# A second way to split weight pieces: casting and adding DMAs for every other piece of the mixer phases

## The chip, the cores and the metric

One NeuronCore of a Trainium2 chip runs the whole program. The metric is the device time of one execution in microseconds (us). Engines are named as in the profile: PE (TensorE, matmuls), PEld (its weight loads, which overlap PE), DVE (VectorE), ACT (ScalarE), POOL (GpSimd) and SP (SyncE). A difference of about 0.2% is what a measurement of this kernel can tell.

## The reference

Two layers of a decoder trunk on 272 tokens (16 meta tokens and 256 of input) and a width of 1024, in float32. Cut to what matters:

```
for l in range(DEPTH):                       # 2 layers
    u = rms_norm(x, norm1_g[l]) @ w_in[l]    # 1024 x 6560
    (u_conv, c_q, c_kv, k_rope, hq, hf, hi, hg, u_gate) = split(u)
    y_a = conv_module(u_conv, ...)           # gated causal depthwise conv, layer norm, swish, projection
    y_b = mla(c_q, c_kv, k_rope, ...)        # latent attention, 8 heads, projection
    y_c = hgrn2(hq, hf, hi, hg, ...)         # gated linear recurrence, 4 heads, projection
    mix = gates[0] * y_a + gates[1] * y_b + gates[2] * y_c
    x = x + mix @ w_out[l]
    x = x + square(relu(rms_norm(x, norm2_g[l]) @ w_ff1[l])) @ w_ff2[l]
```

## The kernel before

Activations lie transposed in SBUF (features on partitions, tokens along the row). All the large products run on PE with both operands split into a high and a low part of type float32r; `mm3` (L218) adds three matmuls, high x high, low x high and high x low. The weights come as **pieces** of 128 x 1024 float32 (512 KB): one piece feeds 8 steps of 128 rows, 24 matmuls of up to 272 columns. There are 276 of them.

`piece` (L204) fetches a piece by a DMA on SP's queue into `wraw` (3 buffers, `fetch`, L104), rounds it on ACT into `whi` (L209, 4 buffers) and takes the difference on DVE into `wlo` (L211, 4 buffers). A slot of `whi` and `wlo` comes free when the last matmul that reads the piece has run. `piece` raises the priority of these steps by 500, so the planner of the language puts them as early as buffers allow. The planner lays out the order of every engine's queue ahead of time by its own simulated times; each engine then works its queue strictly in order.

Each layer has a mixer phase and a feed-forward phase. In the mixer phase a hand-written list `dense` (L1008) sets the order of weight products: tiles of `w_in` by `win_acc` (L367), first 7 latent pieces (j below NLAT = 8), then the head tiles to j = 27, then 24 gate tiles; with the last gate tiles the `merge_tile` products (L982) alternate, each piece of the branch projections (`wbr`) serving two of them. Between these, four streams of smaller steps (latent, HGRN, attention, convolution) are woven in at set rates (L1015 to L1028). They use DVE and ACT heavily, and POOL for a few things: powers of -0.5 for norms (`rsqrt`, L238, and L912), clearing `kl` (L799) and copying `qm` (L851). Pieces of `wuq` and `wukv` go through the same four slots. The evacuations of PSUM go over ACT (L412 to L435, L980) and DVE (L996); `win_acc` uses two PSUM banks `acc`, in the latent part `hx` too. The feed-forward phase (L1038 to L1095), `wout`, `wff1` and `wff2`, uses 72 pieces in each layer.

Of the kernel before, what the change touches and what calls it, by code (L numbers as in the profile page):

```python
# [10 lines left out]
F32 = mybir.dt.float32  # L11
# [3 lines left out]
AF = mybir.ActivationFunctionType  # L15
# [24 lines left out]
NLAT = 8  # L40
# [46 lines left out]
def block_kernel(ctx, tc, xT_d, pp_d, cc_d, win_d, wuq_d, wukv_d, wbr_d, wout_d, wff1_d, wff2_d, out_d):  # L87
    nc = tc.nc
    pe, act, dve, pool = nc.tensor, nc.scalar, nc.vector, nc.gpsimd
    MUL, ADD, SUB = ALU.mult, ALU.add, ALU.subtract  # L90
# [13 lines left out]
    def fetch(src, n=1024):  # L104
        raw = wsp.tile([P, 1024], F32, name="wraw", tag="wraw")
        nc.sync.dma_start(out=raw[:, :n], in_=src[:, :n])
        return raw
# [3 lines left out]
    with tc.high_priority(offset=2 * AHEAD):  # L111
        nc.scalar.dma_start(out=pp, in_=pp_d)
        for j in range(4):
            nc.sync.dma_start(out=xT[:, 2 * j:2 * j + 2, :], in_=xT_d[:, 2 * j:2 * j + 2, :])
            if j == 0:
                first = {"kr": fetch(win_d[0, 0], KD * ROPE), "kv": fetch(win_d[0, 1])}
# [72 lines left out]
    def psum_acc():  # L189
        return ps_acc.tile([P, 512], F32, name="acc", tag="acc")  # L190
# [4 lines left out]
    def psum_hx():  # L195
        return ps_hx.tile([P, 512], F32, name="hx", tag="hx")
# [4 lines left out]
    def psum_sm():  # L201
        return ps_sm.tile([P, 512], F32, name="sm", tag="sm")

    def piece(src, raw=None):  # L204

        with tc.high_priority(offset=AHEAD):
            raw = raw or fetch(src)
            hi = wsp.tile([P, 1024], F32R, name="whi", tag="whi", bufs=4)
            act.copy(out=hi, in_=raw)  # L209
            lo = wsp.tile([P, 1024], F32R, name="wlo", tag="wlo", bufs=4)  # L210
            dve.tensor_tensor(out=lo, in0=raw, in1=hi.bitcast(F32), op=SUB)  # L211
        return hi, lo

    def split(hi, lo, src):
# [3 lines left out]
    def mm3(out, whi, wlo, xhi, xlo, start, stop):  # L218
        pe.matmul(out, whi, xhi, start=start, stop=False)  # L219
        pe.matmul(out, wlo, xhi, start=False, stop=False)  # L220
        pe.matmul(out, whi, xlo, start=False, stop=stop)  # L221
# [62 lines left out]
    def scale_input(xg, l, k):  # L284
# [16 lines left out]
                      in1=lb[:, 5, :].unsqueeze(1).broadcast_to([P, 2, HH]), op=MUL)  # L301
# [5 lines left out]
    for l in range(DEPTH):  # L307
# [33 lines left out]
        def unit(name, dt=F32):  # L341
            return t4.tile([P, HH, L], dt, name=name, tag="u")
# [22 lines left out]

        tiles = win_tiles()
        def win_acc(j, n0):  # L367
            hi, lo = piece(win_d[l, j], first["kv"] if l == 0 and j == 1 else None)
            xh, xl = xg if j < NLAT else (hhi, hlo)
            ps = psum_hx() if j < NLAT and j % 2 == 0 else psum_acc()  # L370
            for k in range(KD):
                o = k * P
                mm3(ps[:, :L - n0], hi[:, o:o + P], lo[:, o:o + P], xh[:, k, n0:], xl[:, k, n0:],
                    k == 0, k == KD - 1)
            return ps
# [22 lines left out]
        def head_tile(j):  # L398
            kind, i, _, _ = tiles[j]
            if kind == "kr":  # L400
                rope_keys(j)
                return
            n0 = T0 if kind in ("q", "g") else 0
            ps = win_acc(j, n0)[:, :L - n0]
            with tc.high_priority(offset=200):
                take(kind, i, ps, n0)
# [40 lines left out]
        def latent_steps():  # L447
# [44 lines left out]
            for g in range(2):  # L492
                uqhi, uqlo = piece(wuq_d[l, g])
                for h in range(4):
                    ps = psum_mx()[:, :L]
                    for j in range(2):
                        o = j * 512 + h * P
                        mm3(ps, uqhi[:, o:o + P], uqlo[:, o:o + P], cqhi[:, j, :], cqlo[:, j, :], j == 0, j == 1)
                    act.activation(out=msq_[:QK, h, :], in_=ps[:QK], func=AF.Square)
                    dve.tensor_tensor(out=qT[g][:, h, :], in0=ps, in1=csg, op=MUL)  # L500
                    yield
                with together():
                    for h in (3, 2, 1, 0):
                        pe.matmul(sums[32 * h:32 * h + 32, :L], sel96[:QK, g, :], msq_[:QK, h, :], start=(g == 0), stop=(g == 1))
                yield
# [3 lines left out]
            for w in qtiles:  # L509
# [10 lines left out]
                                     in1=heads(ra[:, 1, q0:3]), op0=MUL, op1=MUL)  # L520

            ukhi, uklo = piece(wukv_d[l])
            kT = [unit(f"kT{g}") for g in range(2)]
            vv = [half(f"vv{w}", "vv", 3) for w in range(3)]
# [449 lines left out]
        mix = {}  # L974

        def gate_tile(i):

            ps = win_acc(N_HEAD_TILES + i, T0)
            gates[i] = gp.tile([P, L], F32, name="gate", tag="gate")
            act.activation(out=gates[i][:, :N], in_=ps[:, :N], func=AF.Tanh, scale=0.5)  # L980

        def merge_tile(i):  # L982
            b, m = divmod(i, KD)
            yh, yl = ys[BRANCHES[b]]
            if i == 0:
                mix["sum"] = [unit(f"mix{j}") for j in range(2)]
            if i % 2 == 0:
                mix["w"] = piece(wbr_d[l, i // 2])
            bhi, blo = mix["w"]
            ps = (psum_acc, psum_hx, psum_hx)[b]()  # L990
            for k in range(4):
                o = (i % 2 * 4 + k) * P
                mm3(ps[:, :N], bhi[:, o:o + P], blo[:, o:o + P], yh[:, k, T0:], yl[:, k, T0:], k == 0, k == 3)
            g, total = gates[i], mix["sum"][m // 4][:, m % 4, :N]
            with tc.high_priority(offset=AHEAD):
                dve.scalar_tensor_tensor(out=total if b == 0 else g[:, :N], in0=g[:, :N], scalar=1.0, in1=ps[:, :N], op0=ADD, op1=MUL)  # L996
            if b > 0:
                dve.tensor_tensor(out=total, in0=total, in1=g[:, :N], op=ADD)  # L998
            if b == 2:
                if m == 0:  # L1000
                    mix["hi"] = actp.tile([P, KD, L], F32R, name="mhi", tag="ahi")
                    mix["lo"] = actp.tile([P, KD, L], F32R, name="mlo", tag="alo")
                act.activation(out=mix["hi"][:, m, T0:], in_=total, func=AF.Copy, scale=0.5)
                dve.scalar_tensor_tensor(out=mix["lo"][:, m, T0:], in0=total, scalar=0.5, in1=mix["hi"][:, m, T0:].bitcast(F32),
                                         op0=MUL, op1=SUB)
# [3 lines left out]
        for i in range(3 * KD):  # L1009
            dense.append((merge_tile, i))  # L1010
            if i + NGATE < 3 * KD:
                dense.append((gate_tile, i + NGATE))
# [193 lines left out]
```

## Time and profile before

| | us |
|---|---|
| median of 3 runs | 961.36 (961.18 to 961.63) |
| the profiled execution | 961.29 |
| its span, first to last instruction | 959.5 |
| PE busy | 931.0 |
| DVE busy | 716.5 |
| ACT busy | 526.3 |
| POOL busy | 50.7 |

Busy time counts an engine's instructions, not its waits. In a group of lines, "idle before" is the time for which the engine stood just before these instructions, with what ended it; in a timeline the same stands in square brackets. PE's matmuls are pipelined, so a matmul's own duration (about 290 ns) overlaps the next; some 0.12 us lie between two starts. Granted clock 1.00 is TensorE's full clock.

The kernel's phases can be told by the stretch: up to about 280 us the first layer's mixer phase, to about 482 its feed-forward phase, to about 760 the second mixer phase, then the second feed-forward phase.

### The profile page before, as it was taken

The numbers are of one execution on the slowest core, as the hardware profiler recorded it, in microseconds if no ns is written. First come the engines' busy times: TensorE is split into PE (matmuls) and PEld (weight loads), VectorE is DVE, ScalarE is ACT, GpSimd is POOL, SyncE is SP. The second block draws the span as 40 slices with busy tenths as digits, with TensorE's granted clock in tenths as the row PEclk, the third lists the DMA queues.
The fourth block names the chain that finished last, engine by engine and source line by source line (L and its number), as shares of the span: only waits on it lengthen the run. The fifth ranks groups of instructions, "written<-read, shape, count | busy, mean of one in ns | idle before, by whom it ended". The sixth has DMA issues, their size and how long they took to land. (4 is left out here: it accounts for less than half of the span.)

```text
span 959.5 us, 18623 instructions
## 1 busy us (share of the span) xinstructions
PE 931.0 (97%) x7474; PEld 896.2 (93%) x7474; DVE 716.5 (75%) x1348; ACT 526.3 (55%) x945; POOL 50.7 (5%) x87
## 2 busy tenths in 40 slices
PE   6999999899999999999999999997998999999998
PEld 6899999779999999999999889896897999999998
DVE  7799999976887766555557998999668887665552
ACT  6467665554546555544445587665444566663331
POOL 3004000000000000000010021000000000000000
PEclk9999999989999999999999999998999999999999
DMA  8454433414445555555454444333144466555661
GB/s 264 131 176 140 147 133 111 133 34 142 163 148 178 194 176 177 176 176 176 160 172 158 141 145 155 130 132 113 67 146 163 155 195 199 179 190 187 198 203 56
DMA packets 42422, 149.16 MB, mean 155 GB/s; under 512 B 4704, under 2 KB 6368, under 8 KB 42336
## 3 DMA queue, kind: packets, MB, share of 16 engines
q1 hardware_dynamic: 40608, 146.10, 46.2%
q10 hardware_dynamic: 1728, 1.88, 0.6%
q8 instruction: 58, 0.95, 0.4%
q14 instruction: 28, 0.23, 0.1%
HBM read 146.91 MB, written 1.05 MB: 154 GB/s over the span
## 5 line engine op out<-in xcount | busy, mean ns | idle before, releaser
L209 ACT CAST whi<-wraw 128x1024 fp32r<-128x1024 f32 x276 | 289.3, 1049 | 340.4 <-PE acc L221 191.2
L211 DVE TENSOR_TENSOR wlo<-wraw,whi 128x1024 fp32r<-128x1024 f32 x276 | 337.6, 1223 | 167.0 <-ACT whi L209 165.4
L219 PE MATMUL acc<-hhi,whi 128*128 128x272 f32 (+1 forms) x704 | 205.1, 292 | 2.3 <-ACT scrahi L417 1.6
L221 PE MATMUL acc<-hlo,whi 128*128 128x272 f32 (+1 forms) x704 | 202.7, 289 | 0.2 <-DVE hlo L216 0.2
L220 PE MATMUL acc<-hhi,wlo 128*128 128x272 f32 (+1 forms) x704 | 202.2, 287 | 0.0
L219 PEld LDWEIGHTS acc<-hhi,whi 128*128 128x128 f32 x704 | 132.6, 188 | 6.6 <-ACT scrahi L417 1.8
L221 PEld LDWEIGHTS acc<-hlo,whi 128*128 128x128 f32 x704 | 132.4, 188 | 2.5 <-issue 0.9
L220 PEld LDWEIGHTS acc<-hhi,wlo 128*128 128x128 f32 x704 | 132.6, 188 | 1.2 <-issue 0.4
L935 DVE SCALAR_TENSOR_TENSOR cacc<-hpad,pph,cacc 128x272 f32<-128x272 f32 (+1 forms) x240 | 111.0, 485 | 0.7
L220 PE MATMUL acc<-xhi,wlo 128*128 128x272 f32 (+1 forms) x256 | 73.4, 287 | 0.0
L220 PE MATMUL hx<-xhi,wlo 128*128 128x272 f32 (+1 forms) x256 | 73.2, 286 | 0.0
L221 PE MATMUL acc<-xlo,whi 128*128 128x272 f32 (+1 forms) x256 | 73.1, 286 | 0.0
L221 PE MATMUL hx<-xlo,whi 128*128 128x272 f32 (+1 forms) x256 | 72.9, 285 | 0.0
L220 PE MATMUL hx<-fhi,wlo 128*128 128x272 f32 (+1 forms) x256 | 72.9, 285 | 0.0
L220 PE MATMUL acc<-fhi,wlo 128*128 128x272 f32 (+1 forms) x256 | 72.9, 285 | 0.0
L219 PE MATMUL acc<-fhi,whi 128*128 128x272 f32 (+1 forms) x256 | 72.8, 284 | 0.0
L219 PE MATMUL hx<-fhi,whi 128*128 128x272 f32 (+1 forms) x256 | 72.8, 284 | 0.0
L221 PE MATMUL acc<-flo,whi 128*128 128x272 f32 (+1 forms) x256 | 72.7, 284 | 0.0
L221 PE MATMUL hx<-flo,whi 128*128 128x272 f32 (+1 forms) x256 | 72.7, 284 | 0.0
L219 PE MATMUL acc<-xhi,whi 128*128 128x272 f32 (+1 forms) x256 | 72.7, 284 | 0.0
L219 PE MATMUL hx<-xhi,whi 128*128 128x272 f32 (+1 forms) x256 | 72.7, 284 | 0.0
L221 PEld LDWEIGHTS acc<-xlo,whi 128*128 128x128 f32 x256 | 48.3, 189 | 0.1
(375 smaller groups left out, 2097.3 us busy)
## 6 DMA issues: line engine op xcount, KB each, us to landing
wraw<-in_wff_dram SPq DMA_DIRECT2D x128, 512.0 KB, 3.4
wraw<-in_win_dram SPq DMA_DIRECT2D x102, 512.0 KB, 3.4
wraw<-in_wbr_dram SPq DMA_DIRECT2D x24, 512.0 KB, 3.3
wraw<-in_wout_dram SPq DMA_DIRECT2D x16, 512.0 KB, 3.3
wraw<-in_wuq_dram SPq DMA_DIRECT2D x4, 512.0 KB, 3.2
xT<-in_xT_dram SPq DMA_DIRECT2D x4, 272.0 KB, 5.4
wraw<-in_wukv_dram SPq DMA_DIRECT2D x2, 512.0 KB, 3.7
out_dram<-xT ACTq DMA_DIRECT2D x8, 128.0 KB, 2.4
```

The lines of the kernel that those rows point to most:

```text
L209: act.copy(out=hi, in_=raw)
L211: dve.tensor_tensor(out=lo, in0=raw, in1=hi.bitcast(F32), op=SUB)
L219: pe.matmul(out, whi, xhi, start=start, stop=False)
L220: pe.matmul(out, wlo, xhi, start=False, stop=False)
L221: pe.matmul(out, whi, xlo, start=False, stop=stop)
L935: dve.scalar_tensor_tensor(out=a, in0=hpad[:, c, T0 + k:T0 + k + N], scalar=hpar(l, "cw", c * CK + k), in1=a, op0=MUL, op1=ADD)
```

## The change

`piece` gets a flag. With it, the piece isn't fetched into `wraw`: a DMA on POOL's queue reads the float32 weights from HBM and writes them as float32r into `whi` (a cast), ACT writes the negative of `whi` into `wlo`, and a second DMA on POOL's queue reads the same weights again and adds them to `wlo`. The flag is set for odd j from 9 on in `win_acc` (22 pieces in a layer) and for every second `wbr` piece (6 in a layer), 56 of 276 pieces. All others are made as before.

```diff
-    def piece(src, raw=None):
+    def piece(src, raw=None, adding=False):
         with tc.high_priority(offset=AHEAD):
-            raw = raw or fetch(src)
             hi = wsp.tile([P, 1024], F32R, name="whi", tag="whi", bufs=4)
-            act.copy(out=hi, in_=raw)
             lo = wsp.tile([P, 1024], F32R, name="wlo", tag="wlo", bufs=4)
-            dve.tensor_tensor(out=lo, in0=raw, in1=hi.bitcast(F32), op=SUB)
+            if adding:
+                nc.gpsimd.dma_start(out=hi, in_=src)
+                act.activation(out=lo, in_=hi.bitcast(F32), func=AF.Copy, scale=-1.0)
+                nc.gpsimd.dma_start(out=lo, in_=src, accum_op=ADD)
+            else:
+                raw = raw or fetch(src)
+                act.copy(out=hi, in_=raw)
+                dve.tensor_tensor(out=lo, in0=raw, in1=hi.bitcast(F32), op=SUB)
         return hi, lo
...
-            hi, lo = piece(win_d[l, j], first["kv"] if l == 0 and j == 1 else None)
+            hi, lo = piece(win_d[l, j], first["kv"] if l == 0 and j == 1 else None, j >= NLAT and j % 2 == 1)
...
-                mix["w"] = piece(wbr_d[l, i // 2])
+                mix["w"] = piece(wbr_d[l, i // 2], adding=i % 4 == 2)
```

## Rows read from the trace of the kernel before

**Rows 1.** The page: span, and busy us (share), instructions, by engine.
```profile
span 959.5 us, 18623 instructions
...
PE 931.0 (97%) x7474; PEld 896.2 (93%) x7474; DVE 716.5 (75%) x1348; ACT 526.3 (55%) x945; POOL 50.7 (5%) x87
```

**Rows 2.** Busy time by stretch, from the span's start; clock, DMA share, GB/s.
```profile
84.00:172.00 88.00, 88.00 (x720) 83.45 (x720) 82.70 (x199) 55.36 (x128) 6.33 (x8) 1.00 0.40 133
172.00:206.00 34.00, 28.51 (x212) 23.91 (x211) 29.88 (x79) 19.07 (x49) 1.29 (x2) 0.90 0.24 77
...
276.00:480.00 204.00, 204.00 (x1623) 203.92 (x1622) 130.22 (x187) 105.41 (x162) 0.00 (x0) 1.00 0.53 174
...
507.00:562.00 55.00, 53.44 (x414) 49.64 (x413) 47.65 (x102) 36.19 (x59) 6.14 (x3) 1.00 0.42 137
...
658.00:684.00 26.00, 20.44 (x152) 16.34 (x152) 20.90 (x55) 13.33 (x34) 0.63 (x1) 0.80 0.17 60
684.00:752.00 68.00, 64.18 (x524) 61.39 (x523) 50.10 (x90) 30.49 (x48) 2.71 (x3) 1.00 0.45 149
```

**Rows 3.** PE's timeline around the longest hole of each layer: start, duration.
```profile
191.29 1.12 PE L844 MATMUL hx<-q,k 128*64 128x64 f32 x8 [3.28 <-DVE k L840]
...
666.89 1.12 PE L844 MATMUL hx<-q,k 128*64 128x64 f32 x8 [2.81 <-DVE k L840]
```

**Rows 4.** Busy time in short stretches at these holes; the clock stands third from last.
```profile
186.00:190.00 4.00, 0.96 (x5) 0.57 (x5) 4.00 (x13) 2.60 (x8) 0.29 (x1) 1.00 0.16 36
190.00:198.00 8.00, 6.24 (x36) 4.46 (x36) 8.00 (x25) 4.16 (x14) 0.00 (x0) 0.57 0.14 50
664.00:676.00 12.00, 7.61 (x44) 5.55 (x43) 10.91 (x32) 4.58 (x14) 0.63 (x1) 0.57 0.12 44
```

**Rows 5.** Costliest groups (the two of `piece`), and the cast's waits (us, times, longest).
```profile
L211 DVE TENSOR_TENSOR wlo<-wraw,whi 128x1024 fp32r<-128x1024 f32 x276 | 337.6, 1223 | 167.0 <-ACT whi L209 165.4
L209 ACT CAST whi<-wraw 128x1024 fp32r<-128x1024 f32 x276 | 289.3, 1049 | 340.4 <-PE acc L221 191.2 <-PE hx L221 97.0 <-issue 37.5
...
ACT whi L209 <- PE acc L221: 191.2, 129, 4.2
...
ACT whi L209 <- DMA wraw<-in_win_dram: 3.7, 4, 1.2
```

**Rows 6.** L106: all fetches; those of 84 to 172 us; landing times, all, then that stretch.
```profile
L106 SPq DMA_DIRECT2D wraw<-in_win_dram x104: 327/328/487, 1.2 to 707.5; - x104
...
DMA to landing us min/median/max: 2.8/3.4/6.6
...
DMA to landing us min/median/max: 3.1/3.3/3.9
```

**Rows 7.** POOL's timeline from 60 to 260 us: start, duration, idle before.
```profile
72.62 2.90 POOL L238 TENSOR_TENSOR ks<-ks,mhalf 128x8 f32<-128x8 f32 x1 [26.33 <-DVE ks L557]
...
85.00 1.64 POOL L238 TENSOR_TENSOR ks<-ks,mhalf 128x8 f32<-128x8 f32 x1 [1.85 <-DVE rq L519]
...
186.39 0.29 POOL L851 COPY qm<-q 128x128 f32<-128x128 f32 x1 [16.84 <-DVE q L839]
```

**Rows 8.** Timelines of ACT and PE: two pieces' casts and their first matmuls.
```profile
222.22 1.05 ACT L209 CAST whi<-wraw 128x1024 fp32r<-128x1024 f32 x1 [2.37 <-PE acc L221]
...
228.61 0.39 PE L219 MATMUL acc<-hhi,whi 128*128 128x272 f32 x1
...
97.66 1.04 ACT L209 CAST whi<-wraw 128x1024 fp32r<-128x1024 f32 x1 [0.58 <-PE acc L221]
...
110.38 0.37 PE L219 MATMUL acc<-hhi,whi 128*128 128x272 f32 x1
```

**Rows 9.** Line 209 alone by stretch: length, ACT busy and casts, clock, DMA share, GB/s.
```profile
84.00:172.00 88.00, 23.07 (x22) 1.00 0.40 133
...
206.00:276.00 70.00, 21.00 (x20) 1.00 0.43 144
...
562.00:658.00 96.00, 27.87 (x27) 1.00 0.42 143
...
684.00:752.00 68.00, 20.01 (x20) 1.00 0.45 149
```

**Rows 10.** The first layer's wukv piece on PE: duration min/median/max, first and last start.
```profile
L541 PE MATMUL hx<-whi,kvm x1: 398/398/398, 62.5 to 62.5; 128*128 128x512 f32 x1
...
L543 PE MATMUL hx<-wlo,mla_hi x2: 392/446/499, 64.6 to 84.3; 128*128 128x512 f32 x2
```

## The prediction

> **What bounds the kernel now.** I read the page's busy table first [rows 1]: PE is busy 931.0 of 959.5 us, DVE 716.5, ACT 526.3, POOL 50.7. The reader is to see that PE is nearly the whole span, so no change off PE gives much unless it closes a hole in PE. The profiled execution took 961.29 us, 1.8 us more than its span; the median of the runs is 961.36, so sums made against the profile carry over as they are.
>
> The busy table by stretch shows where holes are [rows 2]. In 84 to 172 us PE never rests, but DVE works 82.7 of 88 us. In 172 to 206 PE loses 5.5 us, in 658 to 684 5.6, in 684 to 752 3.8 and in 507 to 562 1.6: 16.5 us in all. What ends PE's wait is DVE: the longest is 3.28 us before L844, released by DVE L840, and its twin in the second layer 2.81 us [rows 3]. Around each the granted clock, 1.00 (2.4 GHz) before, falls towards 0.50 (1.2 GHz): its mean is 0.57 over 8 us and over 12 us [rows 4], so 0.43 x 20 = 8.6 us of PE's work is lost to the clock. All that a lighter DVE can give back is thus some 16.5 + 8.6 = 25 us.
>
> Last I looked at the weight ring. The groups of lines give 276 casts (L209, 1049 ns) and 276 subtractions (L211, 1223 ns) [rows 5]. The commonest wait of the cast is on PE's L221, 191.2 us in 129 times: the cast waits for a slot of whi to be given back, not for its DMA, for which the first such row has 3.7 us [rows 5]. So the ring of four is full, and a piece has from the release of its slot until PE reaches it. I call that its room.
>
> **The change, part by part.** 28 pieces per layer change (22 of win, 6 of wbr), 56 of 276.
>
> Removed: 56 x 1.223 = 68.5 us of DVE, all in the mixer phases, and 56 fetches from SP's queue. Replaced one for one: the cast on ACT by a scaled copy of the same size, 1.05 us; I count it at nothing, because ACT has 33 of 88 us free in the fullest stretch [rows 2]. If that cover were gone it would cost a few tenths each.
>
> Gain: of the 25 us I take half, 12 us. The holes stand behind DVE chains whose own length stays, but the 1.2 us subtractions and the backlog that stand between their links become fewer. Bounds: 0 (the chains stay as long) and 25 us. What is late next is PE's own work, or the weights.
>
> Added, and the heart of it: a chain that starts only when a slot is free. Before, raw was fetched ahead into its own three buffers, and from a free slot it took 1.05 + 1.22 us to a ready piece. Now it is DMA to hi, negation on ACT, adding DMA to lo, one behind the other. The trace of before shows no DMA issued by POOL, no casting and no adding one. Lower bound: two plain fetches of the same 512 KB at 3.3 us, and 1.05 us of ACT: 7.7 us [rows 6]. Upper bound: a fetch that had company took up to 6.6 us, and each of the two is issued by POOL, whose small instructions take up to 1.6 us and in cases more where SP's issue takes 0.33; 2 x (6.6 + 1.6) + 1.05 is 17.5 us [rows 6, 7]. I take 11.5: 1.0 us on POOL and 3.4 to land; 1.5 for ACT with its queue; 1.0 on POOL and 4.6 to land, since an adding DMA has two operands to read and lies somewhere between one fetch (3.3) and two (6.6). It is nearer to the lower end because its nearest row is the plain fetch of the same bytes, and because there is room on the DMA engines: 28 more reads of 0.52 MB in a layer's some 260 us are 56 GB/s on top of 133 to 149, about 200, where the feed-forward phase carries 174 at a share of 0.53 without a hole [rows 2].
>
> On the issue the Trainium skill, DMA: Bandwidth & Descriptors, section Latency and other measured facts, gives about 1 us to the first byte for a DMA issued by GpSimd against 0.6 on the hardware path. No run here shows it; an estimate by that page alone adds 0.8 us to the lower bound, 8.5 us, and by it the loss below would be 11 us.
>
> What the chain meets: the room. I read it for the 56 pieces in the timelines of ACT and PE, from the cast that takes the slot to the first matmul of the piece. Shortest is the piece of 222.22, first used at 228.61, 6.4 us; a usual one of the long stretch is that of 97.66, used at 110.38, 12.7 us [rows 8]. The count of casts per stretch tells why: 22 in 88 us is one every 4.0 us, three of them 12.0; in 206 to 276 one per 3.5 us, in 684 to 752 one per 3.4 us [rows 9], and there two pieces are used alternately, so that some have hardly two periods. From 62.5 us the piece of wukv holds one slot for 22 us, to 84.3 [rows 10], and the room is 7 to 10; layer 1 has the same around 540.
>
> A piece that comes late moves all after it, and the next adding piece has that much more room; so about one of two stalls. Going through the 56 in order with a chain of 11.5 us, PE stands 7.2 us in 44 to 84, 0.6 in 84 to 172, 15.2 in 206 to 280, 4.7 in 507 to 562, 4.1 in 562 to 658 and 14.6 in 684 to 760: 46 us. The same with other lengths: 5.5 us at 7.7, 14 at 9, 25 at 10, 80 at 13, 132 at 15, 197 at 17.5. If the planner spreads the work evenly, only the averages count: four pieces in one turn need 11.5 us and the 24 matmuls of one piece (24 x 88/720 = 2.9), 14.4 us, and have 16.0 (84 to 172), 14.2, 14.0 and 13.6; that loses 0, 2, 2 and 4 us, with the two held-slot stretches 20 us. I take 35, between the two and nearer to the first, since the uneven places are made by the order of the merge.
>
> Added waits: on ACT, the negation waits for a landing, and casts, tanh evacuations and exponentials are queued behind it; PE waits for them with two acc buffers. On POOL, every DMA waits for a slot or for ACT, and behind it stand the rsqrts (L238, L912), the clears of kl and the copies of qm; DVE waits for those. In the other direction a DMA stands behind a POOL instruction that waits for DVE, up to 17 us of idling before one [rows 7]. Bounds 0 (the planner's order fits) and the upper chain; I take 6 us. Stalls of over 3 us also pull the clock down, as the two holes do; two such are lost with the gain and some new ones come: 3 us, between 0 and 27 (the eight of over 3 us at 0.43 x 8 = 3.4).
>
> Sum: 961.3 - 12 + 35 + 6 + 3 = **993 us**.
>
> **The rivals.** *Short chain, faster:* place, the 56 chains; price, 68.5 us of DVE against little; it decides where the chain is under 8.8 us, at which loss equals gain. With 8.2 us and no queueing the time is 961.3 - 12 + 8 = 957; with all 25 us gained 945. For it speaks 3.3 us as the ordinary landing [rows 6]; against it, that adding needs a second read and that POOL issues.
>
> *Long chain:* POOL's part stretches while DVE works. For it: the same rsqrt on 128x8 took 2.90 us at 72.62 and 1.64 at 85.00 [rows 7]. If each of the two DMAs is 1.3 us later, the chain is 14 us, the loss 106 and the time 961.3 - 12 + 106 + 9 = 1064. The Trainium skill, SBUF — State Buffer, section Who interferes with whom, has a rule of this kind: DVE in a two-port mode shuts GpSimd out of the port by which it writes descriptors. Whether it bears on these DVE instructions no row shows.
>
> *The change does not bind:* the planner gives adding pieces their slots earlier, and the chains are hidden: gain and loss both small, within 0.2% of 961.
>
> **How the numbers follow.** The forecast (chain 10 to 13 us, with gain and waits away from my values 965 to 1035) gets 0.50. Long chain or POOL's order (1035 to 1130) gets 0.25: it is a matter of 2.5 us on two operations that I have not seen. Short chain gets 0.20, most of it faster; hidden 0.05. The measurement can tell about 0.2% (1.9 us). Faster 0.17, within 0.2% 0.07, slower 0.76. For 8 in 10 the range takes in most of the short and the lower part of the long chain: 953 to 1085.
>
> **What would show it.** In the profile after: POOL's DMA to landing, 4.4 us for whi and 5.6 for wlo by my split; DVE busy lower by 68 us; new waits of PE's L220 on DMA wlo, most of them in the merge (206 to 280 and its twin); the holes before L844 shorter. I am wrong if PE's waits on wlo total under 10 us or over 90, or if PE waits mainly for ACT's evacuations or for POOL's rsqrts rather than for weights.

## The result and the profile after

The changed kernel takes 1042.14 us in the median (1039.06 to 1044.21), the kernel before 961.27 in the same comparison: a ratio of 1.0832, interval 1.0817 to 1.0847. It is 81 us slower, where the forecast was 32 us slower; 1042 lies inside the range. The profiled execution of after took 1041.59 us with a span of 1039.5.

Line numbers move: L211 is now the casting DMA, L212 the negation, L213 the adding DMA, L216 the cast and L217 the subtraction; the three matmuls L219 to L221 are L225 to L227, and L844 is L850.

The page of the kernel after: span; busy us by engine; the two DMA queues that carry weights (packets, MB, share of 16 engines); HBM; the chain by engine and by line; DMA issues with the median us to landing. Its first lines answer to [rows 1].

```profile
span 1039.5 us, 18668 instructions
...
PE 958.1 (92%) x7474; PEld 917.5 (88%) x7474; DVE 657.2 (63%) x1292; ACT 526.4 (51%) x945; POOL 133.9 (13%) x199
...
q1 hardware_dynamic: 32544, 116.73, 34.3%
q0 software_dynamic: 16128, 58.73, 25.4%
...
PE 66%; issue 16%; DMA 11%; ACT 4%; POOL 2%; DVE 1%; POOLq 0%; ACTq 0%
PE acc L226 12%; PE acc L225 12%; PE acc L227 12%; PE hx L226 8%; PE hx L227 8%; PE hx L225 8%; DMA wlo<-in_win_dram 6%; DMA whi<-in_win_dram 3%; DMA wlo<-in_wbr_dram 1%; POOL wlo L213 1%; POOL whi L211 1%; PE mx L640 1%; ACT whi L216 1%; ACT wlo L212 1%; PE hx L816 0%
...
wraw<-in_win_dram SPq DMA_DIRECT2D x58, 512.0 KB, 4.2
whi<-in_win_dram POOLq DMA_DIRECT2D x44, 512.0 KB, 4.8
wlo<-in_win_dram POOLq DMA_DIRECT2D x44, 512.0 KB, 6.0
...
whi<-in_wbr_dram POOLq DMA_DIRECT2D x12, 512.0 KB, 6.2
wlo<-in_wbr_dram POOLq DMA_DIRECT2D x12, 512.0 KB, 5.7
```

Two subtractions of numbers in this block and in [rows 1] split the whole loss. PE stands still for 1039.5 - 958.1 = 81.4 us, where it stood 959.5 - 931.0 = 28.5: 53 us more. And the same 7474 matmuls take 958.1 us where they took 931.0: 27 us more, although not one of them was changed. Nearly all of the second part is the clock: the mean granted clock of the run is 0.969 against 0.991, and 0.031 x 1039.5 - 0.009 x 959.5 = 24 us. DVE is busy for 59 us less; what that brings can't be told from this sum and is measured below.

Where PE stands, by stretch: length, PE busy, PEld, DVE, ACT, POOL, clock, DMA share, GB/s. It answers to [rows 2]; the phases have moved, so the stretches differ.

```profile
84.00:172.00 88.00, 84.78 (x682) 77.64 (x680) 74.50 (x209) 59.92 (x146) 26.19 (x30) 1.00 0.66 167
...
232.00:310.00 78.00, 61.57 (x446) 58.74 (x447) 33.47 (x64) 27.12 (x41) 12.40 (x18) 0.91 0.70 176
310.00:514.00 204.00, 204.00 (x1623) 203.92 (x1622) 130.22 (x187) 105.42 (x162) 0.00 (x0) 1.00 0.54 174
...
760.00:835.00 75.00, 57.07 (x399) 54.50 (x398) 32.31 (x67) 24.38 (x38) 10.15 (x14) 0.86 0.62 161
```

The reader is to see that the feed-forward phase, which the change does not touch, is what it was (204.00 of 204), that the long stretch of the first layer loses 3 us, and that the merge, 232 to 310 and its twin 760 to 835, loses 16.4 and 17.9 us and most of the clock. The DMA engines are busy for 0.66 of the long stretch at 167 GB/s, where the feed-forward phase has 0.54 at 174.

What PE waits for in the kernel after: us in total, times, longest.

```profile
PE acc L226 <- DMA wlo<-in_win_dram: 39.6, 19, 7.2
PE hx L226 <- DMA wlo<-in_wbr_dram: 8.6, 3, 4.2
PE hx L401 <- DVE wkr L397: 7.4, 1, 7.4
PE acc L226 <- DMA wlo<-in_wbr_dram: 4.3, 3, 2.4
PE acc L225 <- ACT scrahi L423: 3.7, 4, 2.0
PE acc L225 <- ACT gate L986: 2.9, 2, 2.3
```

52.5 us in 25 waits are for the landing of the low part, at the second matmul of a piece (L226). The wait of L395 on DVE, now L401, was there before with 7.3. The holes before L844 [rows 3] are gone: L850 has no row in this view.

One piece on its way, in the timeline of the kernel after from 234 to 249 us: start, duration, engine and line, idle before and what ended it.

```profile
234.46 0.55 POOL L211 DMA_DIRECT2D whi<-in_win_dram  x1 [2.32 <-PE acc L227]
...
240.33 1.06 ACT L212 ACTIVATE wlo<-whi 128x1024 fp32r<-128x1024 f32 x1 [1.23 <-DMA whi<-in_win_dram]
...
241.68 0.86 POOL L213 DMA_DIRECT2D wlo<-in_win_dram  x1 [6.67 <-ACT gate L986]
...
248.42 0.39 PE L226 MATMUL acc<-hhi,wlo 128*128 128x272 f32 x1 [2.04 <-DMA wlo<-in_win_dram]
```

POOL issues the casting DMA 0.3 us after PE's last matmul has given the slot back. 5.9 us later ACT negates, at 241.68 POOL issues the adding DMA, and 6.7 us after that PE, which has stood for 2.04 us, goes on. From the slot to the landed piece that is 14.2 us.

I read this chain for all 56 pieces. From the free slot to the issue it takes 0.6 us on average, the casting DMA 5.4 to land, ACT comes 0.6 later and works 1.06, POOL issues the adding DMA 0.4 later, and that takes 6.3 to land: 14.2 us. In 31 of the 56 pieces PE takes up the low part within 0.1 us of its landing, and 25 waits stand in the view above, so about one of two stalls. The landings of the two tiles (us, least, median, most, wlo and then whi) bear out the two large terms:

```profile
DMA to landing us min/median/max: 5.2/5.8/8.9
...
DMA to landing us min/median/max: 3.5/5.0/8.8
```

### The profile page after: what moved, and what is told of

Same layout as the page of the kernel before. It is cut to its first block, busy times and chain, and to the rows that moved or that the text cites. A ratio compares the mean times of both kernels' runs of the same rounds, so it can differ in the third digit from the quotient of the medians.

```text
span 1039.5 us, 18668 instructions
## 1 busy us (share of the span) xinstructions
PE 958.1 (92%) x7474; PEld 917.5 (88%) x7474; DVE 657.2 (63%) x1292; ACT 526.4 (51%) x945; POOL 133.9 (13%) x199
## 3 DMA queue, kind: packets, MB, share of 16 engines
q0 software_dynamic: 16128, 58.73, 25.4%
## 4 chain that ended last, share of the span: by engine, by line
PE 66%; issue 16%; DMA 11%; ACT 4%; POOL 2%; DVE 1%; POOLq 0%; ACTq 0%
PE acc L226 12%; PE acc L225 12%; PE acc L227 12%; PE hx L226 8%; PE hx L227 8%; PE hx L225 8%; DMA wlo<-in_win_dram 6%; DMA whi<-in_win_dram 3%; DMA wlo<-in_wbr_dram 1%; POOL wlo L213 1%; POOL whi L211 1%; PE mx L640 1%; ACT whi L216 1%; ACT wlo L212 1%; PE hx L816 0%
## 5 line engine op out<-in xcount | busy, mean ns | idle before, releaser
L217 DVE TENSOR_TENSOR wlo<-wraw,whi 128x1024 fp32r<-128x1024 f32 x220 | 269.2, 1224 | 207.2 <-ACT whi L216 206.6
L216 ACT CAST whi<-wraw 128x1024 fp32r<-128x1024 f32 x220 | 230.2, 1047 | 287.2 <-PE acc L227 132.0
L226 PE MATMUL acc<-hhi,wlo 128*128 128x272 f32 (+1 forms) x704 | 212.9, 303 | 39.7 <-DMA wlo<-in_win_dram 39.6
L225 PE MATMUL acc<-hhi,whi 128*128 128x272 f32 (+1 forms) x704 | 214.0, 304 | 9.9 <-ACT scrahi L423 3.7
L227 PE MATMUL acc<-hlo,whi 128*128 128x272 f32 (+1 forms) x704 | 209.9, 300 | 0.0
L226 PEld LDWEIGHTS acc<-hhi,wlo 128*128 128x128 f32 x704 | 141.0, 201 | 46.7 <-DMA wlo<-in_win_dram 45.3
L225 PEld LDWEIGHTS acc<-hhi,whi 128*128 128x128 f32 x704 | 141.2, 201 | 16.2 <-ACT scrahi L423 4.6
L227 PEld LDWEIGHTS acc<-hlo,whi 128*128 128x128 f32 x704 | 140.6, 201 | 2.3 <-issue 0.6
L212 ACT ACTIVATE wlo<-whi 128x1024 fp32r<-128x1024 f32 x56 | 59.3, 1060 | 81.1 <-DMA whi<-in_win_dram 50.3
L226 PE MATMUL acc<-xhi,wlo 128*128 128x272 f32 (+1 forms) x256 | 73.4, 287 | 0.0
L226 PE MATMUL hx<-xhi,wlo 128*128 128x272 f32 (+1 forms) x256 | 73.2, 286 | 0.0
L227 PE MATMUL acc<-xlo,whi 128*128 128x272 f32 (+1 forms) x256 | 73.1, 286 | 0.0
L226 PE MATMUL hx<-fhi,wlo 128*128 128x272 f32 (+1 forms) x256 | 72.9, 285 | 0.0
L226 PE MATMUL acc<-fhi,wlo 128*128 128x272 f32 (+1 forms) x256 | 72.9, 285 | 0.0
L227 PE MATMUL hx<-xlo,whi 128*128 128x272 f32 (+1 forms) x256 | 72.9, 285 | 0.0
L225 PE MATMUL hx<-fhi,whi 128*128 128x272 f32 (+1 forms) x256 | 72.9, 285 | 0.0
L225 PE MATMUL acc<-fhi,whi 128*128 128x272 f32 (+1 forms) x256 | 72.9, 285 | 0.0
L227 PE MATMUL acc<-flo,whi 128*128 128x272 f32 (+1 forms) x256 | 72.8, 284 | 0.0
L225 PE MATMUL acc<-xhi,whi 128*128 128x272 f32 (+1 forms) x256 | 72.8, 284 | 0.0
L227 PE MATMUL hx<-flo,whi 128*128 128x272 f32 (+1 forms) x256 | 72.8, 284 | 0.0
L225 PE MATMUL hx<-xhi,whi 128*128 128x272 f32 (+1 forms) x256 | 72.7, 284 | 0.0
```

The source lines that it names most:

```text
L212: act.activation(out=lo, in_=hi.bitcast(F32), func=AF.Copy, scale=-1.0)
```

## Experiments

**The theory.** The chain from a free slot to a landed low part, 14.2 us, is longer than the room which a ring of four slots leaves a piece, so PE stands; its parts are the two DMAs and the negation. **The rivals:** that the extra transfers as such slow everything (their bytes, an adding DMA as traffic); that what is queued behind the waiting instructions on ACT and POOL costs; that DVE's relief is worth less than taken.

Below, "standing" is span less PE's busy time, and "matmuls" PE's busy time over the 931.0 of before; both are differences of page lines as above, from the profiled execution, while the times are medians. The profiled execution of e11_change_in_long_rooms took 7 us less than its median and that of e7_slots5 5 us more, so their two columns lean that way.

| kernel | us | ratio, interval | standing | matmuls |
|---|---|---|---|---|
| before | 961.3 | | 28.5 | 0 |
| after | 1042.1 | 1.0832, 1.0817 to 1.0847 | 81.4 | +27.1 |
| e1_quarter | 1010.1 | 1.0514, 1.0474 to 1.0554 | 57.3 | +21.1 |
| e2_no_subtraction | 942.6 | 0.9803, 0.9788 to 0.9818 | 14.5 | -4.9 |
| e3_cast_no_add | 981.9 | 1.0219, 1.0185 to 1.0252 | 42.4 | +7.2 |
| e4_negate_on_pool | 1111.1 | 1.1556, 1.1522 to 1.1589 | 123.1 | +55.0 |
| e5_whi5 | 994.0 | 1.0338, 1.0314 to 1.0363 | 52.2 | +7.3 |
| e6_before_whi5 | 961.8 | 1.0003, 0.9993 to 1.0012 | 25.7 | +2.1 |
| e7_slots5 | 1006.8 | 1.0480, 1.0453 to 1.0507 | 61.1 | +17.3 |
| e8_before_slots5 | 978.3 | 1.0172, 1.0157 to 1.0187 | 36.9 | +7.9 |
| e9_cast_only | 991.1 | 1.0309, 1.0293 to 1.0325 | 47.6 | +8.4 |
| e10_add_only | 970.8 | 1.0100, 1.0086 to 1.0114 | 33.8 | +6.9 |
| e11_change_in_long_rooms | 981.5 | 1.0192, 1.0158 to 1.0227 | 37.3 | +4.2 |
| e12_add_only_long_rooms | 953.6 | 0.9909, 0.9896 to 0.9922 | 19.6 | -1.9 |

### What the removed subtractions are worth

The 56 subtractions go; the fetch and ACT's cast stay, and no DMA is added. The low part of these pieces is left out: the high part stands in its place in the matmuls, so they take no `wlo` slot either.

```diff
-            lo = wsp.tile([P, 1024], F32R, name="wlo", tag="wlo", bufs=4)
+            lo = None if adding else wsp.tile([P, 1024], F32R, name="wlo", tag="wlo", bufs=4)
             if adding:
-                nc.gpsimd.dma_start(out=hi, in_=src)
-                act.activation(out=lo, in_=hi.bitcast(F32), func=AF.Copy, scale=-1.0)
-                nc.gpsimd.dma_start(out=lo, in_=src, accum_op=ADD)
+                raw = raw or fetch(src)
+                act.copy(out=hi, in_=raw)
+                lo = hi
```

> The 56 pieces are fetched and cast as before, the subtraction on DVE is left out and the low part is not computed: the high part stands in its place in the matmuls. It takes the 68 us off DVE and adds no DMA, so it shows the gain of a lighter DVE by itself. My prediction's term: 12 us, between 0 and 25: 949 us (936 to 961). Rival (the holes stand behind DVE chains that stay as long, as the holes of after were filled by others): at most 3 us, 958 to 961.

942.6 us, 18.5 less than before in this comparison (961.1). 14 us of it is standing and 5 the matmuls. Its PE waits have no row of L850 any more, and none on weights. So DVE's relief is real, and larger than the 12 us taken. The `wlo` slots that these pieces leave free are a second difference, which this run does not separate; PE had no wait for weights before either, so it can hardly be worth much. The loss against this kernel is 1042.1 - 942.6 = 99.5 us, and all of it has to come from how the pieces are made.

### Half as many pieces

```diff
-            hi, lo = piece(win_d[l, j], ..., j >= NLAT and j % 2 == 1)
+            hi, lo = piece(win_d[l, j], ..., j >= NLAT and j % 4 == 1)
...
-                mix["w"] = piece(wbr_d[l, i // 2], adding=i % 4 == 2)
+                mix["w"] = piece(wbr_d[l, i // 2], adding=i % 8 == 2)
```

> Only every fourth piece of the mixer phases (11 + 3 in a layer, 28 in all) goes over casting and adding DMAs; the rest as before. Theory (chain against room): an adding piece stands PE still when its chain of about 14 us is longer than what the ring of four slots gives it, and one stall gives the next adding piece that much more room, so that about one of two stalls now. One per turn of the ring stalls nearly as often in all: 65 to 100% of the 81 us lost, 1014 to 1042 us. Rival (a price for each piece: DMA traffic, ACT's or POOL's queue): half of the loss, 1001 us, give or take 8.

1010.1, which lies between the two intervals, in neither. Half of the pieces cost 49 of the 81 us. Their chain is shorter (12.1 us from issue to landing where after has 13.6, with the high part landing in 4.2), yet PE waits 34.8 us for the low part (19.7 and 15.1), 1.24 us a piece where after has 52.5 / 56 = 0.94. The waits are 15, again one for about two pieces, where the theory had nearly as many as the 25 of after. A cost proportional to the bytes or to the number of DMAs would have halved, to 1001 us; 9 us above that is little more than the margin of 8 which was given to the rival, so this run alone decides little.

### The second DMA without the adding

The second DMA overwrites the low part, so that it is not the low part; all else stays, the order and the bytes moved too.

```diff
-                nc.gpsimd.dma_start(out=lo, in_=src, accum_op=ADD)
+                nc.gpsimd.dma_start(out=lo, in_=src)
```

> The second DMA writes the weights over the low part instead of adding them to it, so that the low part is wrong by the negative high part; all queues, waits and HBM reads stay. It shows the price of the adding. In the trace of after the adding DMA lands in 5.8 us (median) from its issue and the casting one in 5.0. Theory (chain against room): landing some 0.8 us sooner, chain 13 us instead of 14, PE's waits fewer by 10 to 20 us with the clock's: 1022 to 1034 us. Rival (adding itself is the cause, by reading the destination): landing at 4 us or less, time under 1005.

981.9 us: 60 of the 81 us are gone. That is far below the 1022 to 1034 of the theory, which took the landing to be 0.8 us sooner, and under the 1005 of the rival, adding itself, whose landing of 4 us or less is nearly met. The page of this kernel, the queue of POOL's DMAs and the landings of two of them:

```profile
q0 software_dynamic: 16128, 58.73, 18.8%
...
whi<-in_win_dram POOLq DMA_DIRECT2D x44, 512.0 KB, 4.6
wlo<-in_win_dram POOLq DMA_DIRECT2D x44, 512.0 KB, 4.2
```

Packets and bytes of q0 are those of after, but their time falls from 25.4% of a span of 1039.5 to 18.8% of 980.6, from 264 to 184 us: adding costs engine time that overwriting does not. The low part lands in 4.2 us on average over the 56 where it took 6.3, and the high part, which is the same instruction as in after, in 4.6 where it took 5.4. From the free slot the chain is 11.3 us. The overwriting kernel moves as many bytes and makes the same number of issues, so neither of these is what costs; the adding is. Whether by the 2.9 us of chain or by its load on the DMA engines, this run can't tell, since it changes both; e5_whi5 below changes the room alone.

The Trainium skill, Collectives: The Full Stack, section The bandwidth ceiling: the fold count and why AG ≠ RS ≠ AR, says of ReduceScatter, a transfer between cores that adds, that it runs at about half the rate of AllGather, which copies, because the add needs two source reads. Here the landing grew by half, 6.3 against 4.2, so the direction agrees. The time on the DMA engines comes nearer to the double: the queue has 94 us for 56 casting DMAs in e9_cast_only and 168 us for 56 adding ones in e10_add_only, further down.

### The negation moved to POOL

```diff
-                act.activation(out=lo, in_=hi.bitcast(F32), func=AF.Copy, scale=-1.0)
+                pool.tensor_scalar(out=lo, in0=hi.bitcast(F32), scalar1=-1.0, scalar2=None, op0=MUL)
```

> The negation moves from ACT to POOL; nothing else changes. Theory (chain against room): ACT no longer waits for a landing, but the chain stays as long or gets longer by the slower engine: 1035 to 1065 us. Rival (ACT's queue: casts and evacuations stand behind a negation that waits for its DMA, 81 us in all in the trace of after): most of the loss goes, 965 to 1000 us.

1111.1 us, above what was expected. ACT is relieved of the waits, and nothing is gained. The negation's line in this kernel (count, least, median and most ns):

```profile
L212 POOL TENSOR_SCALAR wlo<-whi x56: 2762/2780/7695, 33.0 to 887.0; 128x1024 fp32r<-128x1024 f32 x56
```

It takes 2.6 times as long as on ACT in the median, and the low part's landings grow too, from 6.3 to 6.8 us on average. PE now waits 73.5 us for the low part (52.5, 13.2 and 7.8). From issue to landing the chain is 16.9 us where it was 13.6, and the time is longer by 69 us. That fits a price for the chain's length and speaks against the rival of ACT's queue. It is not a clean measure of the length: DVE is busy for 678.3 us here where after has 657.2, and the wait now stands on POOL's queue, ahead of the next pieces' DMAs.

### More room for the same chain

A fifth slot for the high part (for both parts in e7_slots5). The space comes from the gate buffers, hence the two controls, which are the kernel before with the same numbers.

```diff
-NGATE = 15
+NGATE = 13
...
-            hi = wsp.tile([P, 1024], F32R, name="whi", tag="whi", bufs=4)
+            hi = wsp.tile([P, 1024], F32R, name="whi", tag="whi", bufs=5)
```

> The changed kernel with a fifth whi buffer (wlo stays at four; the memory for it comes from 13 gate buffers instead of 15). The casting DMA may start one piece earlier, some 3.5 us of more room, with the same DMAs, queues and instructions. Theory (chain against room): as if the chain were 10.5 us instead of 14; in the run without the adding a chain of 10.7 us lost 21 us against before, so 970 to 990 us. Rival (DMA traffic or the adding as such): no change, 1035 to 1050 us.

> Control: the kernel before with the same buffers (five whi, 13 gates). Its pieces are ready some 8 us ahead of use, so more room should give nothing: 958 to 963 us by every theory.

994.0 us, 48 of the 81 recovered and a little less than expected; the control is unchanged at 961.8. The chain is as long as before (13.8 us from issue to landing, after 13.6), while the time from issue to PE's first matmul of the piece, with the pieces taken in their order, is some 16 us where it was some 12. PE's waits for the low part fall from 52.5 to 28.1 us:

```profile
PE acc L226 <- DMA wlo<-in_win_dram: 17.8, 11, 4.2
PE hx L226 <- DMA wlo<-in_wbr_dram: 9.9, 4, 3.9
...
PE acc L226 <- DMA wlo<-in_wbr_dram: 0.4, 1, 0.4
```

So the same DMAs with the same bytes cost far less if the ring is longer: it is chain against room.

```diff
-NGATE = 15
+NGATE = 9
...
-            hi = ... bufs=4
-            lo = ... bufs=4
+            hi = ... bufs=5
+            lo = ... bufs=5
```

> The changed kernel with five whi and five wlo buffers and only 9 gate buffers. Theory (chain against room): both halves of the chain get a piece more room; 965 to 990 us unless fewer gate buffers cost something, which the control shows. Rival (traffic, adding as such): 1035 to 1050.

> Control: the kernel before with five whi, five wlo and 9 gate buffers: 955 to 970 us by every theory; what it is over 961 is the price of the fewer gate buffers.

1006.8 against its control of 978.3. Six gate buffers less cost the kernel before 17 us, which was not expected, and the change adds 28.5 on top, little less than one more slot of the high part alone leaves over its own control (32.2). A fifth slot of the low part brings hardly anything beside the gate buffers that it needs.

### The two DMAs one by one

The casting DMA alone: the high part comes by it, the raw piece is fetched as well, and DVE subtracts as before.

```diff
             if adding:
+                raw = fetch(src)
                 nc.gpsimd.dma_start(out=hi, in_=src)
-                act.activation(out=lo, in_=hi.bitcast(F32), func=AF.Copy, scale=-1.0)
-                nc.gpsimd.dma_start(out=lo, in_=src, accum_op=ADD)
+                dve.tensor_tensor(out=lo, in0=raw, in1=hi.bitcast(F32), op=SUB)
```

> The casting DMA alone: it brings hi, while the float32 weights are fetched by SP too and DVE makes the low part by subtraction as before. No negation, no adding DMA. Theory (chain against room): hi lands some 3.5 us after its issue, since no adding DMA stands before it on POOL's queue; with the subtraction the chain is 5 to 6 us, under every piece's room (6.4 us and up), and DVE has all its work: 955 to 965 us. Rival (a DMA issued by POOL is late or in the way as such, also by its second read of the weights): over 975.

991.1 us, 29 more than before: a miss, since I expected no loss from a chain of some 6 us, and the time is where the rival had it. The casting DMA lands in 4.8 us on average, not in 3.5, although no adding DMA stands on POOL's queue in this kernel. The waits (L213 is here the subtraction of the 56 pieces; us, times, longest) tell what I had not counted:

```profile
DVE wlo L213 <- DMA whi<-in_win_dram: 27.6, 16, 4.6
...
DVE wlo L213 <- DMA whi<-in_wbr_dram: 13.7, 6, 5.1
...
PE hx L850 <- DVE k L846: 12.2, 2, 7.4
...
PE hx L225 <- DVE gate L1002: 10.9, 4, 5.0
```

The subtraction stands at the head of DVE's queue until the casting DMA has landed, 41 us in all, and the chains of DVE that PE needs stand behind it: the hole before L850, 3.28 and 2.81 us before [rows 3], is now 12.2 in two. PE has hardly any wait for weights, so the landing stops it only by way of DVE. The loss has another path here than in after: a wait put on the engine which has the least time to spare, DVE [rows 2].

The adding DMA alone: fetch and cast as before, negation, adding DMA.

```diff
-                nc.gpsimd.dma_start(out=hi, in_=src)
+                raw = raw or fetch(src)
+                act.copy(out=hi, in_=raw)
```

> The adding DMA alone: hi is made as before by a fetch on SP's queue and a cast on ACT, then ACT writes the negative and the adding DMA makes the low part; DVE is as light as in the changed kernel, HBM reads are the same, ACT has 56 x 1.05 us more. Theory (chain against room): from the slot 1.05 + 1.06 + 0.4 + 5.8 = 8.3 us, and no casting DMA queues behind an adding one; by the piece-by-piece table 8 to 11 us lost against a gain of 18.5: 948 to 958 us. Rival (adding DMAs load the engines, whatever the chain): over 970.

970.8 us, above the theory's interval and where the rival's begins. Lines are one further here (L227 is after's L226). POOL's queue in e9_cast_only and then in this kernel, 56 casting DMAs and 56 adding ones:

```profile
q0 software_dynamic: 8064, 29.36, 9.5%
...
q0 software_dynamic: 8064, 29.36, 17.3%
```

That is 9.5% of a span of 987.0, 94 us, and 17.3% of 971.7, 168 us: for the same packets and bytes an adding DMA takes 1.8 times the time of a casting one on the DMA engines. Landings in this kernel and PE's two waits on them:

```profile
wlo<-in_win_dram POOLq DMA_DIRECT2D x44, 512.0 KB, 5.5
...
wlo<-in_wbr_dram POOLq DMA_DIRECT2D x12, 512.0 KB, 7.2
```

```profile
PE acc L227 <- DMA wlo<-in_win_dram: 11.6, 7, 3.4
...
PE hx L227 <- DMA wlo<-in_wbr_dram: 2.7, 3, 2.1
```

Taking the casting DMA out of the chain is thus worth 1042.1 - 970.8 = 71 us, though its share of the chain is only some 6 us; without it, chain and room nearly meet. Still 28 us over the kernel without subtractions, where the table of the prediction gave 8 to 11; PE's waits for the low part are half of that, and how much the adding DMAs' load on the engines has in the rest is not separated.

### Where the room is long

The change on the 13 odd pieces 19 to 43 of win in each layer and on none of wbr, and then the adding DMA alone on the same pieces.

```diff
-            hi, lo = piece(win_d[l, j], ..., j >= NLAT and j % 2 == 1)
+            hi, lo = piece(win_d[l, j], ..., 19 <= j <= 43 and j % 2 == 1)
...
-                mix["w"] = piece(wbr_d[l, i // 2], adding=i % 4 == 2)
+                mix["w"] = piece(wbr_d[l, i // 2], adding=False)
```

> The change as it is, but only for 13 win pieces in a layer (odd j from 19 to 43), where the room before was 9 to 14 us, and for no wbr piece. Theory (chain against room): the chain stays near 14 us there, since the pieces follow each other as closely; by the piece-by-piece table 34 us lost, and 26/56 of the gain of 18.5: 975 to 1000 us. Rival (a price for each piece): 26/56 of the 81 us, 999 us; shorter than 970 would speak against both.

> The adding DMA alone, as in the run before last, only for the 13 win pieces in a layer with long rooms. Theory (chain against room): 8.3 us is under every one of these rooms, so nothing is lost and 26/56 or more of the gain of 18.5 us stays: 947 to 954 us. Rival (adding DMAs load the engines): slower than 961.

981.5 and 953.6 us, both as expected; the first interval, 975 to 1000, held its rival's 999 too, and 981.5 is 18 us under that. With the whole chain, PE waits 17.7 us for 26 pieces even there. With the adding DMA alone:

```profile
PE hx L402 <- DVE wkr L398: 6.5, 1, 6.5
PE hx L226 <- DVE gate L1003: 2.7, 4, 0.9
PE acc L227 <- DMA wlo<-in_win_dram: 2.3, 2, 1.5
```

The low part still takes 6.0 us to land, but PE's waits on it total 2.3 us, and 8.4 us are gained, nearly all of what 26 of 56 pieces can bring by e2_no_subtraction (18.5 x 26 / 56 = 8.6). This kernel is faster than both, by 0.9% (0.8 to 1.0) than the one before.

## Why the prediction was right and wrong

**The mechanism, right.** The chain begins at the free slot and is weighed against the room; that is what e5_whi5 shows (same chain, more room), and e3_cast_no_add (shorter chain) and e4_negate_on_pool (longer chain), which change other things too, agree. PE waits at the second matmul of a piece on the low part, about one piece in two stalls, most of the loss is in the merge, the group of subtractions shrinks by 68.4 us (337.6 [rows 5] to 269.2; the durations of all of DVE's instructions add up to 68 us less, and the page's busy time, which counts instructions that overlap once, falls by 59) and the holes before L844 vanish: all as the prediction said it would show.

**The chain, mis-sized: 11.5 us where 14.2 were measured.** The high part was taken at 1.0 + 3.4 = 4.4 and is 0.6 + 5.4 = 6.0. ACT's part was taken at 1.5 and is 1.6. The adding DMA was taken at 1.0 + 4.6 = 5.6 and is 0.4 + 6.3 = 6.7, its landing near the longest of a fetch in company, 6.6 [rows 6]. POOL's issues, for which I kept a full 1 us twice, take 0.53 to 1.03 and count within the landing; the landings were the larger error. I had argued from free DMA engines that a landing stays near the plain 3.4. What I left out is what an adding DMA does to the others in flight. I grouped the landings of after: the 34 casting DMAs issued within 5 us after an adding one land in 6.1 us on average, the other 22 in 4.3. This is not a matter of POOL's queue: of the plain fetches of win and wbr, which are on SP's queue, the 30 issued within 5 us after an adding DMA land in 5.6 us and the other 42 in 3.8. With overwriting in place of adding (e3_cast_no_add) the two are 4.8 and 4.2 for the casting DMAs, 4.2 and 3.8 for the fetches. So the adding slows DMAs of both queues, which fits its longer time on the engines. It is not all: in e9_cast_only, with no adding DMA, the casting one still takes 4.8.

**The standing for it: 35 taken, 54 measured** (52.5 for the low part, 1.5 for the high part). The prediction's own rules at 14.2 us give more than was measured. By averages, four pieces need 14.2 + 2.9 = 17.1 us a turn and have 16.0, 14.2, 14.0 and 13.6, which over 5.5, 6.75, 5 and 5 turns is 59 us, with 12 or more for the held slots 71. Piece by piece it is 111. So the step that failed first is the chain's length; at the true length 35 would have been wrong by either rule. But the rules failed too, the other way: with the right chain they give at least 17 us more than was measured, and that 35 is not further off is luck, as the two errors partly cancel.

**The clock, mis-sized: 3 us taken, 27 measured against the kernel before, 32 against the one without subtractions.** The prediction counted a few stalls of over 3 us at 3.4 each. Only four of the 25 waits for the low part are longer than that (3.1 to 7.2); they are 2.1 us on average and more than half of their time lies in the merge; there the granted clock, a mean of its levels of 2.4 and 1.2 GHz, is 0.91 and 0.86 over 78 and 75 us, where the kernel before had 0.57 in two stretches of 8 and 12 us [rows 4]. Half-speed matmuls in 232 to 310 and 760 to 835 alone cost 0.09 x 78 + 0.14 x 75 = 17.5 us. In the table of runs the matmuls' excess goes only roughly with the standing: 55 us at 123, 27 at 81, but 21 at 57 and 7 at 52; none below 20. Which pattern of stalls lowers the clock can't be told from these runs.

**DVE's gain: 12 taken, 18.5 measured** by e2_no_subtraction, inside the bounds 0 to 25. The prediction put all 16.5 us of the holes down to DVE; some 6 of them were PE's waits for ACT (L669, L699, L713 and scrahi), and most of these are gone in that run as well. **Queued waits: 6 taken, 6 measured:** PE waits for ACT's evacuations (scrahi, gate, qq) 8.2 us where it was 2.1; no wait of PE is for POOL's rsqrts, and DVE's own waits for POOL are 4 us in all where they were 6. (The longest idling of POOL before an instruction that waits for DVE, 17 us in the prediction, is 26.33 in [rows 7].) But this term is small only because of where the waits stand: on DVE the landing of the casting DMA alone costs 29 us against the kernel before, which has the same subtractions (e9_cast_only).

**With the right sizes** the sum is 961.3 - 18.5 + 54 + 32 + 6 = 1035, 7 short of 1042; the rest are short gaps that I did not assign. The clock stands here with 32 us, since the 18.5 already hold the 4.9 us by which the matmuls were faster without subtractions.

**The rivals.** The short chain would have needed under 8.8 us; even e3_cast_no_add with 11.3 is 21 us slower than before, and its loss of 39 us against e2_no_subtraction is near the 43 that the piece-by-piece table gives for 11.3, between its 25 at 10 and its 46 at 11.5. The long chain, 14 us and 1064, had the right chain and was 22 us too high: its 106 us of standing were 54, and the clock's larger loss made up for about half of that. But its reason was wrong. It rested on a POOL that is slowed by DVE. The issues never took more than 1.03 us. The rule of the Trainium skill that went with it (SBUF — State Buffer, section Who interferes with whom), by which DVE can shut GpSimd out of the port that writes descriptors, finds no example among POOL's DMA issues of this kernel. "Does not bind" fell with the 25 waits.

**Piece by piece, as a guide.** That table's loss is close to the whole loss against e2_no_subtraction, standing and slower matmuls together: 111 against 99.5 (after), 43 against 39 (e3_cast_no_add). In e10_add_only it is not: 8 to 11 against 28. Standing alone is less, 81.4 - 14.5 = 67 and 42.4 - 14.5 = 28. The table knows no clock, so that two of the sums agree is of use and not an explanation; matmuls at half speed lengthen the room, which the table does not know either.

## What to carry to other kernels

When a step is moved to a chain that can only start once a ring slot is free, compare the chain's length from that slot with the time until the slot is used, piece by piece and above all where the consumption is uneven; take each DMA's landing with its neighbours in flight on any queue, not the plain landing, and count the clock beside the standing: here 27 us came on top of 53, in e4_negate_on_pool 55 on 95, in e5_whi5 7 on 24. Then put the slow path only on pieces whose room is longer than the chain, and leave out the half that costs more than it frees: here the adding DMA alone on 26 pieces gained 0.9% where the whole change on 56 lost 8.3%. Ask, too, on which engine the wait for a landing stands: on DVE, which has little time to spare, that of the casting DMA alone cost 29 us (e9_cast_only).

## What the runs showed of the hardware

- An adding DMA of 512 KB from POOL lands in 6.3 us on average (5.2 to 8.9), the same DMA overwriting in 4.2 (3.4 to 5.9). The packets of POOL's queue take 264 us in the mean of the 16 engines with the one and 184 with the other, for the same 16128 packets. Alone on the queue, 56 adding DMAs take 168 us and 56 casting ones 94.
- In after, DMAs issued within 5 us after an adding one land later than the others, on POOL's queue (6.1 us against 4.3) and on SP's (5.6 against 3.8).
- A casting DMA with no adding DMA close before it lands in 4.3 us on average; its shortest is 3.5, where the shortest plain fetch of the kernel before has 2.8 [rows 6]. The prediction cited from the Trainium skill (DMA: Bandwidth & Descriptors, section Latency and other measured facts) a first byte that comes 0.4 us later for a DMA issued by GpSimd. The 0.7 us between the shortest landings go the same way, and no run singles out the first byte.
- POOL takes 0.53 to 0.89 us to issue the casting DMA and 0.85 to 1.03 for the adding one, where SP takes 0.33 for the plain fetch [rows 6].
- The negation of 128x1024 takes 1.06 us on ACT and 2.78 us in the median on POOL (up to 7.7).
- In this kernel two gate buffers can be given for a fifth `whi` slot at no cost (961.8); six for a fifth slot of both parts cost 17 us (978.3).
